# Retrieval look-ups with one operand in a PSUM bank

## Chip, cores and metric

One core of one Trainium2 chip runs the whole program. The metric is the device time of one execution in microseconds, as the median of several runs; lower is better.

## The reference

A decoder trunk of two layers over 256 tokens of width 1024, all in float32. Each layer has a mixer (a short convolution, then attention) and a product-key expert retrieval, which is what matters here:

```python
def chunk(xc):                                   # peer_ffn
    q = (xc @ w_q).reshape(PEER_CHUNK, PEER_HEADS, 2, PEER_HALF)        # 8 heads, 2 sides
    s1 = jnp.einsum('thd,nd->thn', q[:, :, 0], sub_k1)                  # 128 keys a side
    s2 = jnp.einsum('thd,nd->thn', q[:, :, 1], sub_k2)
    v1, i1 = lax.top_k(s1, PEER_TOPK)                                   # 16 of 128
    v2, i2 = lax.top_k(s2, PEER_TOPK)
    cand = (v1[..., :, None] + v2[..., None, :]).reshape(..., 256)
    cidx = (i1[..., :, None] * PEER_NKEYS + i2[..., None, :]).reshape(..., 256)
    top_s, top_pos = lax.top_k(cand, PEER_TOPK)                         # 16 of 256 pairs
    e_idx = jnp.take_along_axis(cidx, top_pos, axis=-1)
    g = jax.nn.softmax(top_s, axis=-1)
    u = u_emb[e_idx]                                                    # 16384 experts
    a = jax.nn.gelu(jnp.einsum('td,thkd->thk', xc, u))
    w = g * a
    return jnp.einsum('thk,thkd->td', w, v_emb[e_idx])
```

## The kernel before

The kernel doesn't gather experts. It multiplies the normed tokens with the whole table of experts, tile by tile, and puts gates on the result that are zero but for the chosen ones. The weights of the whole program form one list of items of 128 x 1024 float32; per layer there are 8 query tiles, then 128 tiles of u (the U stage) and 128 of v (the V stage). For exactness every operand is split into a high part and the remainder (the low part), and three products are summed.

An item passes through five engines. SyncE loads it (`issue`, L136). A u tile is turned by DVE (`turn_to`, L157), ACT rounds it to its high part (L171), POOL subtracts this in two halves of 512 columns to get the low part (`split_to`, L176), and PE multiplies (L880, L881 with the high part, L884 with the low part). There are three buffers of each kind, so a turn, a split and a load wait for the item three places earlier. For v tiles DVE makes the low part and nothing is turned.

The U stage has two halves. In items 0 to 63 (`WIDE`) an item is 24 matmuls of 256 columns into half a bank (L880, L881, L884), and after every odd item ACT evicts the pair's bank through a GELU (L1022). From item 64 on high and low token parts go in one matmul of 512 columns (L878), and the gate products (DVE L1070, L1078, L1092; PE L1085) run beside them, behind a gate in the order of work that opens only after item 63.

While items 0 to 61 run, DVE works out the retrieval in two batches of 128 tokens, called i = 0 and 1. This is written as a queue of side work: `add(cost, ...)` appends an instruction with a declared cost, and after each item `run_side(1.62)` gives 1.62 of credit and emits instructions while their cost is covered. Nearly all of it has line L215, since `add` calls it from there. The order per batch, all in `peer`: the key numbers of the 16 best of each side are cast to float16; numbers of side 1 are made into differences (`df`); five additions make 65 candidate sums (`cand`) from the side scores `v16`; the 16 largest are found with their positions `tp`; a shift by 4, a shift of 15 and a mask make the column within a block (`sh`, `tp[:, i, 1]`); both are cast to float16 (`pf`). Then each position is looked up by a one-hot: two compares of 2048 elements against `st16` and `io16` write `hot[i]`, a product of 4096 elements multiplies it with the table `tab` of key numbers, and `fold` (L939, three times) with a last addition sums over the 16 places. `tables(i)` lets ACT write that table beforehand: 2 x 2048 float16, each key number repeated 16 times (L933 to L935). At the end come the softmax of the gates, and `listed`, in which PE turns the lists (L995) and ACT evicts them (L999, L1000).

Bank `hi4[3]` (the last 2 KB of PSUM of each partition) is free from item 21 until the gate products keep their constants there from item 64 on: `hold` (L1065) copies them as words with a shift by 0, since the copy is to be bit for bit.

Of the kernel before, what the change touches and what calls it, by code (L numbers as in the profile page):

```python
# [12 lines left out]
F16 = mybir.dt.float16  # L13
BF16 = mybir.dt.bfloat16
I32 = mybir.dt.int32
U32 = mybir.dt.uint32
AF = mybir.ActivationFunctionType
OP = mybir.AluOpType
# [20 lines left out]
def trunk_kernel(ctx: ExitStack, tc, x, norm_mix, norm_ffn, conv_w_in, conv_w, conv_w_out,  # L39
# [3 lines left out]
    pe, dve, act, pool, sp = nc.tensor, nc.vector, nc.scalar, nc.gpsimd, nc.sync  # L43
# [15 lines left out]
    xbuf = sb.tile([128, 2560], F32, name="xbuf")  # L59
# [23 lines left out]
    def scratch(off, n):  # L83
        return big[:, off:off + n]
# [129 lines left out]
    def add(c, f, *a, gate=0, **k):  # L214
        side.append((c, lambda: f(*a, **k), gate))  # L215
# [42 lines left out]
    lo4, hi4 = B[0:4], B[4:8]  # L258
# [565 lines left out]
    def peer(l):  # L824
# [1 line left out]
        S = scratch(base, 4096).rearrange("p (b h s n) -> p b h s n", b=2, h=8, s=2)  # L826
        qT = scratch(80 * 256, 2048).rearrange("p (h t) -> p h t", t=256)
        qs = scratch(60 * 256, 1024).rearrange("p (t c) -> p t c", t=2)
        tab = xbuf[:, 0:2048].bitcast(F16).rearrange("p (g a n) -> p g a n", a=16, n=16)
        hot = [scratch(base + 2048 * i, 2048).bitcast(F16).rearrange("p (g a n) -> p g a n", a=16, n=16)  # L830
               for i in range(2)]
        o = base + 4096
        cand = scratch(o, 8 * 66).rearrange("p (h c) -> p h c", c=66)
        o += 528
        v16 = scratch(o, 512).rearrange("p (b h s n) -> p b h s n", b=2, h=8, s=2)
        i16 = scratch(o + 512, 512).bitcast(U32).rearrange("p (b s h n) -> p b s h n", b=2, h=8, s=2)
        if16 = scratch(o + 1024, 256).bitcast(F16).rearrange("p (b s h n) -> p b s h n", b=2, h=8, s=2)
        ts = scratch(o + 1280, 256).rearrange("p (b h n) -> p b h n", b=2, h=8)
        tp = scratch(o + 1536, 512).bitcast(U32).rearrange("p (b s h n) -> p b s h n", b=2, s=2, h=8)
        sh = scratch(o + 2048, 128).bitcast(U32).rearrange("p (h n) -> p h n", h=8)  # L840
        pf = scratch(o + 2176, 128).bitcast(F16).rearrange("p (s h n) -> p s h n", s=2, h=8)
        df = scratch(o + 2304, 64).bitcast(F16).rearrange("p (h n) -> p h n", h=8)
        f15 = scratch(o + 2368, 128).bitcast(U32).rearrange("p (h n) -> p h n", h=8)
        e12 = scratch(o + 2496, 512).rearrange("p (b s n) -> p b s n", b=2, s=2)
        gg = scratch(o + 3008, 256).rearrange("p (b h n) -> p b h n", b=2, h=8)
        gs = scratch(o + 3264, 16).rearrange("p (b h) -> p b h", b=2)
        io16 = scratch(o + 3280, 128).bitcast(F16).rearrange("p (a n) -> p a n", a=16)
        st16 = scratch(o + 3408, 128).bitcast(F16).rearrange("p (a n) -> p a n", a=16)
        kbd = scratch(o + 3536, 256)
# [70 lines left out]
        def topk(groups, cost):  # L920

            for lo in (0, 8):
                for v, m, p in groups:
                    add(cost, dve.max, m[:, lo:lo + 8], v)
                for v, m, p in groups:
                    add(cost, dve.max_index, p[:, lo:lo + 8], m[:, lo:lo + 8], v)
                if lo == 0:
                    for v, m, p in groups:
                        add(cost, dve.match_replace, v, m[:, 0:8], v, NEG)

        def tables(i):

            act.activation(df[:, :, 0:1], if16[:, i, 0, :, 0:1], AF.Copy)  # L933
            act.activation(tab[:, 8:16], if16[:, i, 1, :, :, None].to_broadcast([128, 8, 16, 16]), AF.Copy)
            act.activation(tab[:, 0:8], df[:, :, :, None].to_broadcast([128, 8, 16, 16]), AF.Copy)  # L935

        def fold(i, n):
            v = hot[i].rearrange("p g a n -> p g (a n)")
# [15 lines left out]
        q_out(1)  # L954
        for i in range(2):
            add(0.6, dve.tensor_copy, if16[:, i], i16[:, i])
            add(0.4, dve.tensor_tensor, df[:, :, 1:16], if16[:, i, 0, :, 1:16], if16[:, i, 0, :, 0:15],
                op=OP.subtract)
            for a0, n, first, width in ((0, 1, 0, 16), (1, 2, 16, 8), (3, 4, 32, 4), (7, 8, 48, 2), (15, 1, 64, 1)):
                add(0.4, dve.tensor_tensor,  # L960
                    cand[:, :, first:first + n * width].rearrange("p h (a c) -> p h a c", c=width),
                    v16[:, i, :, 0, a0:a0 + n, None].to_broadcast([128, 8, n, width]),
                    v16[:, i, :, 1, None, 0:width].to_broadcast([128, 8, n, width]), op=OP.add)
            for h in range(0, 8, 4):
                topk([(cand[:, h + a, 0:65], ts[:, i, h + a], tp[:, i, 0, h + a]) for a in range(4)], 0.25)
                if h == 0:
                    add(0.0, tables, i)
            add(0.4, dve.tensor_scalar, sh, tp[:, i, 0], 4, None, op0=OP.logical_shift_right)
            add(0.4, dve.tensor_tensor, sh, f15, sh, op=OP.logical_shift_right)
            add(0.4, dve.tensor_tensor, tp[:, i, 1], tp[:, i, 0], sh, op=OP.bitwise_and)  # L970
            add(0.6, dve.tensor_copy, pf, tp[:, i])
            add(1.4, dve.tensor_tensor, hot[i][:, 0:8], pf[:, 0, :, None, :].to_broadcast([128, 8, 16, 16]),
                st16[:, None].to_broadcast([128, 8, 16, 16]), op=OP.is_ge)
            add(1.4, dve.tensor_tensor, hot[i][:, 8:16], pf[:, 1, :, None, :].to_broadcast([128, 8, 16, 16]),
                io16[:, None].to_broadcast([128, 8, 16, 16]), op=OP.is_equal)
            add(2.5, dve.tensor_tensor, hot[i], hot[i], tab, op=OP.mult)
            for n in (8, 4, 2):
                add(0.3 + 0.14 * n, fold, i, n)
            add(0.6, dve.tensor_tensor, e12[:, i].rearrange("p s (h n) -> p (s h) n", h=8), hot[i][:, :, 0],
                hot[i][:, :, 1], op=OP.add)  # L980
            add(0.5, dve.tensor_tensor, gg[:, i], ts[:, i], ts[:, i, :, 0:1].to_broadcast([128, 8, 16]),
                op=OP.subtract)
        pause()
        add(0.0, act.activation, gg, gg, AF.Exp)
        add(0.8, dve.tensor_reduce, gs, gg, axis=AX.X, op=OP.add)
        add(0.2, dve.reciprocal, gs, gs)
        add(0.8, dve.tensor_tensor, gg, gg, gs[:, :, :, None].to_broadcast([128, 2, 8, 16]), op=OP.mult)
        lists = (B[4][:, 0:256], B[4][:, 256:512], B[5][:, 0:256])

        def listed():  # L990
# [214 lines left out]

    conv_mixer()
    peer(0)
    attn_mixer()
    peer(1)

# [32 lines left out]
```

## Time and profile before

| | |
|---|---|
| median of 3 runs | 1823.19 us (1821.16 to 1823.33) |
| the profiled execution | 1822.49 us; span 1820.7 us |
| busy: PE, PE weight load | 1797.7 us, 1573.6 us |
| busy: DVE, ACT, POOL | 1353.9 us, 894.6 us, 710.7 us |
| granted TensorE clock | 0.998 of full speed |
| U stage, items 0 to 63 | 137 to 334 us and 1053 to 1249 us |

The span runs from the first to the last instruction of the program; the execution's own time has 1.8 us around it. Busy time is the union of an engine's instructions. In the lists of instructions, a bracket at the end of a line is the idle time of the engine before it and who ended it. Instructions of the same kind that follow each other on one engine are merged into one line with a count.

### The profile page before, as it was taken

The numbers are of one execution on the slowest core, as the hardware profiler recorded it, in microseconds if no ns is written. First come the engines' busy times: TensorE is split into PE (matmuls) and PEld (weight loads), VectorE is DVE, ScalarE is ACT, GpSimd is POOL, SyncE is SP. The second block draws the span as 40 slices with busy tenths as digits, with TensorE's granted clock in tenths as the row PEclk, the third lists the DMA queues.
The fourth block names the chain that finished last, engine by engine and source line by source line (L and its number), as shares of the span: only waits on it lengthen the run. The fifth ranks groups of instructions, "written<-read, shape, count | busy, mean of one in ns | idle before, by whom it ended". The sixth has DMA issues, their size and how long they took to land.

```text
span 1820.7 us, 32357 instructions
## 1 busy us (share of the span) xinstructions
PE 1797.7 (99%) x11985; PEld 1573.6 (86%) x11985; DVE 1353.9 (74%) x2183; ACT 894.6 (49%) x1109; POOL 710.7 (39%) x549
## 2 busy tenths in 40 slices
PE   9999999999999999999999999999999999999998
PEld 8979999988888888888788799999888888888886
DVE  4748888788888887555567487887888898875555
ACT  5455445555454444544454554545455544445443
POOL 1048899978820000000200388999888300000000
PEclk9999999999999999999999999999999999999999
DMA  7566655665555555655562675556565555556564
GB/s 210 154 194 188 183 163 168 175 178 168 172 161 183 166 173 183 227 193 194 163 184 86 174 205 169 166 169 183 165 172 167 160 185 174 174 174 228 191 194 138
DMA packets 204581, 321.15 MB, mean 176 GB/s; under 512 B 26221, under 2 KB 157317, under 8 KB 203910
## 3 DMA queue, kind: packets, MB, share of 16 engines
q1 hardware_dynamic: 202006, 312.33, 56.2%
q10 hardware_dynamic: 2416, 6.75, 1.1%
q8 instruction: 94, 1.54, 0.4%
q14 instruction: 65, 0.53, 0.1%
HBM read 315.83 MB, written 3.15 MB: 175 GB/s over the span
## 4 chain that ended last, share of the span: by engine, by line
PE 90%; DVE 4%; DMA 2%; ACT 1%; POOL 1%; issue 1%; SPq 0%; DVEq 0%; ACTq 0%; POOLq 0%
PE psum L485 41%; PE psum L878 13%; PE psum L884 12%; PE psum L880 5%; PE psum L881 5%; PE psum L1085 3%; PE psum L472 3%; PE psum L518 2%; DVE big L215 1%; POOL lo L176 1%; DVE tr L157 1%; PE psum L916 1%; DVE lo L176 1%; DMA raw<-in_conv_w_out_dram 1%; ACT hi L171 1%
## 5 line engine op out<-in xcount | busy, mean ns | idle before, releaser
L176 POOL TENSOR_TENSOR lo<-tr,hi 128x512 fp32r<-128x512 f32 x496 | 652.3, 1348 | 109.4 <-ACT hi L171 104.8
L176 DVE TENSOR_TENSOR lo<-raw,hi 128x1024 fp32r<-128x1024 f32 x316 | 388.1, 1229 | 259.1 <-ACT hi L171 253.1
L171 ACT ACTIVATE hi<-raw 128x1024 fp32r<-128x1024 f32 x331 | 349.7, 1060 | 448.4 <-PE psum L485 365.4
L485 PE MATMUL psum<-hi,x 128*128 128x512 f32 x2208 | 553.0, 392 | 0.7 <-ACT hi L171 0.7
L485 PEld LDWEIGHTS psum<-hi,x 128*128 128x128 f32 x2208 | 409.0, 188 | 82.6 <-ACT hi L171 1.1
L157 DVE STREAM_TRANSPOSE tr<-raw 128x1024 f32<-128x1024 f32 x256 | 316.0, 1234 | 64.2 <-POOL lo L176 38.2
L171 ACT ACTIVATE hi<-tr 128x1024 fp32r<-128x1024 f32 x256 | 270.3, 1058 | 128.4 <-DVE tr L157 113.5
L884 PE MATMUL psum<-x,lo 128*128 128x256 f32 x2048 | 292.0, 283 | 6.2 <-POOL lo L176 6.2
L485 PE MATMUL psum<-lo,x 128*128 128x512 f32 x1104 | 295.2, 389 | 0.4 <-POOL lo L176 0.4
L884 PEld LDWEIGHTS psum<-x,lo 128*128 128x128 f32 x2048 | 273.6, 191 | 18.6 <-POOL lo L176 8.6
L176 POOL TENSOR_TENSOR lo<-raw,hi 128x512 fp32r<-128x512 f32 (+1 forms) x27 | 49.1, 1848 | 609.5 <-ACT hi L171 557.3
L878 PE MATMUL psum<-x,hi 128*128 128x512 f32 x1024 | 263.6, 398 | 0.0
L880 PE MATMUL psum<-x,hi 128*128 128x256 f32 x1024 | 252.7, 284 | 0.8 <-ACT hi L171 0.8
L881 PE MATMUL psum<-x,hi 128*128 128x256 f32 x1024 | 251.1, 283 | 0.0
L485 PEld LDWEIGHTS psum<-lo,x 128*128 128x128 f32 x1104 | 207.1, 188 | 43.9 <-POOL lo L176 0.8
L878 PEld LDWEIGHTS psum<-x,hi 128*128 128x128 f32 x1024 | 183.6, 189 | 33.3
L880 PEld LDWEIGHTS psum<-x,hi 128*128 128x128 f32 x1024 | 196.3, 192 | 1.5 <-ACT hi L171 1.2
L881 PEld LDWEIGHTS psum<-x,hi 128*128 128x128 f32 x1024 | 196.4, 192 | 0.2
L1185 POOL TENSOR_TENSOR big<-xbuf,big 128x256 f32<-128x256 f32 x2 | 1.4, 732 | 383.4 <-DVE rstd L348 383.4
L1070 DVE TENSOR_TENSOR xbuf<-psum,eT 128x1536 f16<-128x1536 f16 x128 | 119.9, 937 | 10.1 <-PE psum L1085 10.1
L1040 ACT ACTIVATE big<-psum 128x512 f32<-128x512 f32 x64 | 38.2, 597 | 125.6 <-PE psum L884 125.6
L1022 ACT ACTIVATE big<-psum 128x512 f32<-128x512 f32 x64 | 38.1, 596 | 115.6 <-PE psum L884 115.5
(164 smaller groups left out, 1573.4 us busy)
## 6 DMA issues: line engine op xcount, KB each, us to landing
raw<-in_peer_u_dram SPq DMA_DIRECT2D x1024, 128.0 KB, 3.0
raw<-in_peer_v_dram SPq DMA_DIRECT2D x256, 512.0 KB, 4.2
raw<-in_conv_w_in_dram SPq DMA_DIRECT2D x96, 128.0 KB, 2.6
raw<-in_attn_w_qkv_dram SPq DMA_DIRECT2D x96, 128.0 KB, 2.7
raw<-in_peer_w_q_dram SPq DMA_DIRECT2D x64, 128.0 KB, 2.9
raw<-in_conv_w_out_dram SPq DMA_DIRECT2D x8, 512.0 KB, 4.2
raw<-in_attn_w_o_dram SPq DMA_DIRECT2D x8, 512.0 KB, 3.7
x_dram<-xbuf ACTq DMA_DIRECT2D x2, 1024.0 KB, 4.8
```

The lines of the kernel that those rows point to most:

```text
L157: dve.transpose(TR[m % 3].rearrange("p b (g i) -> p g b i", g=4), RAW[m % 3].rearrange("p (g m) -> p g m", m=256))
L171: act.activation(HI[m % 3], src, AF.Copy)
L176: eng.tensor_sub(LO[m % 3][:, c], src[:, c], HI[m % 3][:, c])
L472: pe.matmul(banks[c // 2][:, (c % 2) * 256:(c % 2) * 256 + 256], w[:, c * 128:c * 128 + 128], xx[:, b], start=(b == 0 and p == 0 and c % 2 ...
L485: pe.matmul(banks[j], x[:, j // 2 * 128:j // 2 * 128 + 128], w[:, j % 2 * 512:j % 2 * 512 + 512], start=(first and p == 0), stop=(last and ...
L878: pe.matmul(o, w, X2[:, b], start=(b == 0), stop=False, skip_group_check=True)
L880: pe.matmul(o, w, XH[:, b], start=(b == 0), stop=False)
L881: pe.matmul(o, w, XL[:, b], start=False, stop=False)
L884: pe.matmul(o[:, 0:256], lo[:, b * 128:b * 128 + 128], XH[:, b], start=False, stop=(b == 7), skip_group_check=(o.shape[-1] == 512))
L1040: act.activation(A[:, k - 1:k + 1], halves(k, 1), AF.Copy)
L1070: dve.tensor_tensor(HOT[s % 2].rearrange("p b (r k) t -> p b r k t", r=3), numbers[:, None, None].to_broadcast([128, TOK // 2, 3, 64, 2]), ...
L1085: pe.matmul(o, pairs[:, t // 2, :, t % 2], OHG[s % 2][:, a, t // 2, :, t % 2], start=(a == 0), stop=(a == 1))
```

## The change

What is read by several look-ups is copied into bank `hi4[3]`, so that a DVE instruction has one operand in PSUM and one in SBUF: the positions (`picks`), the key numbers (`values`), the scores of the second side (`side1`), the shifts (`sh`) and the reciprocals of the softmax (`gr`). The positions and the key numbers go there as 32-bit words by a shift of 0 (`words`). ACT's table of 4096 float16 gives way to one in which each number stands twice (`vp`, 512 float16): ACT writes 8 x 2 and 8 x 16 x 2 elements of it, DVE the differences, and the product reads the pairs with a broadcast over a middle dimension. `xbuf` holds two of these tables, one a batch.

```diff
--- before.py
+++ after.py
@@ -826,7 +826,7 @@
         S = scratch(base, 4096).rearrange("p (b h s n) -> p b h s n", b=2, h=8, s=2)
         qT = scratch(80 * 256, 2048).rearrange("p (h t) -> p h t", t=256)
         qs = scratch(60 * 256, 1024).rearrange("p (t c) -> p t c", t=2)
-        tab = xbuf[:, 0:2048].bitcast(F16).rearrange("p (g a n) -> p g a n", a=16, n=16)
+        vp = [xbuf[:, 256 * i:256 * i + 256].bitcast(F16).rearrange("p (g a r) -> p g a r", a=16, r=2) for i in range(2)]
         hot = [scratch(base + 2048 * i, 2048).bitcast(F16).rearrange("p (g a n) -> p g a n", a=16, n=16)
                for i in range(2)]
         o = base + 4096
@@ -837,13 +837,17 @@
         if16 = scratch(o + 1024, 256).bitcast(F16).rearrange("p (b s h n) -> p b s h n", b=2, h=8, s=2)
         ts = scratch(o + 1280, 256).rearrange("p (b h n) -> p b h n", b=2, h=8)
         tp = scratch(o + 1536, 512).bitcast(U32).rearrange("p (b s h n) -> p b s h n", b=2, s=2, h=8)
-        sh = scratch(o + 2048, 128).bitcast(U32).rearrange("p (h n) -> p h n", h=8)
         pf = scratch(o + 2176, 128).bitcast(F16).rearrange("p (s h n) -> p s h n", s=2, h=8)
-        df = scratch(o + 2304, 64).bitcast(F16).rearrange("p (h n) -> p h n", h=8)
         f15 = scratch(o + 2368, 128).bitcast(U32).rearrange("p (h n) -> p h n", h=8)
         e12 = scratch(o + 2496, 512).rearrange("p (b s n) -> p b s n", b=2, s=2)
         gg = scratch(o + 3008, 256).rearrange("p (b h n) -> p b h n", b=2, h=8)
         gs = scratch(o + 3264, 16).rearrange("p (b h) -> p b h", b=2)
+
+        sh = hi4[3][:, 0:128].bitcast(U32).rearrange("p (h n) -> p h n", h=8)
+        picks = hi4[3][:, 0:128].bitcast(F16).rearrange("p (s h n) -> p s h n", s=2, h=8)
+        values = hi4[3][:, 128:384].bitcast(F16).rearrange("p (g a r) -> p g a r", a=16, r=2)
+        side1 = hi4[3][:, 384:512].rearrange("p (h n) -> p h n", h=8)
+        gr = hi4[3][:, 384:400].rearrange("p (b h) -> p b h", b=2)
         io16 = scratch(o + 3280, 128).bitcast(F16).rearrange("p (a n) -> p a n", a=16)
         st16 = scratch(o + 3408, 128).bitcast(F16).rearrange("p (a n) -> p a n", a=16)
         kbd = scratch(o + 3536, 256)
@@ -928,11 +932,14 @@
                     for v, m, p in groups:
                         add(cost, dve.match_replace, v, m[:, 0:8], v, NEG)
 
+        def words(dst, src):
+
+            dve.tensor_scalar(dst, src, 0, None, op0=OP.logical_shift_right)
+
         def tables(i):
 
-            act.activation(df[:, :, 0:1], if16[:, i, 0, :, 0:1], AF.Copy)
-            act.activation(tab[:, 8:16], if16[:, i, 1, :, :, None].to_broadcast([128, 8, 16, 16]), AF.Copy)
-            act.activation(tab[:, 0:8], df[:, :, :, None].to_broadcast([128, 8, 16, 16]), AF.Copy)
+            act.activation(vp[i][:, 0:8, 0], if16[:, i, 0, :, 0:1].to_broadcast([128, 8, 2]), AF.Copy)
+            act.activation(vp[i][:, 8:16], if16[:, i, 1, :, :, None].to_broadcast([128, 8, 16, 2]), AF.Copy)
 
         def fold(i, n):
             v = hot[i].rearrange("p g a n -> p g (a n)")
@@ -954,13 +961,14 @@
         q_out(1)
         for i in range(2):
             add(0.6, dve.tensor_copy, if16[:, i], i16[:, i])
-            add(0.4, dve.tensor_tensor, df[:, :, 1:16], if16[:, i, 0, :, 1:16], if16[:, i, 0, :, 0:15],
-                op=OP.subtract)
+            add(0.4, dve.tensor_tensor, vp[i][:, 0:8, 1:16], if16[:, i, 0, :, 1:16, None].to_broadcast([128, 8, 15, 2]),
+                if16[:, i, 0, :, 0:15, None].to_broadcast([128, 8, 15, 2]), op=OP.subtract)
+            add(0.3, dve.tensor_copy, side1, v16[:, i, :, 1])
             for a0, n, first, width in ((0, 1, 0, 16), (1, 2, 16, 8), (3, 4, 32, 4), (7, 8, 48, 2), (15, 1, 64, 1)):
                 add(0.4, dve.tensor_tensor,
                     cand[:, :, first:first + n * width].rearrange("p h (a c) -> p h a c", c=width),
                     v16[:, i, :, 0, a0:a0 + n, None].to_broadcast([128, 8, n, width]),
-                    v16[:, i, :, 1, None, 0:width].to_broadcast([128, 8, n, width]), op=OP.add)
+                    side1[:, :, None, 0:width].to_broadcast([128, 8, n, width]), op=OP.add)
             for h in range(0, 8, 4):
                 topk([(cand[:, h + a, 0:65], ts[:, i, h + a], tp[:, i, 0, h + a]) for a in range(4)], 0.25)
                 if h == 0:
@@ -969,11 +977,15 @@
             add(0.4, dve.tensor_tensor, sh, f15, sh, op=OP.logical_shift_right)
             add(0.4, dve.tensor_tensor, tp[:, i, 1], tp[:, i, 0], sh, op=OP.bitwise_and)
             add(0.6, dve.tensor_copy, pf, tp[:, i])
-            add(1.4, dve.tensor_tensor, hot[i][:, 0:8], pf[:, 0, :, None, :].to_broadcast([128, 8, 16, 16]),
+            add(0.3, words, hi4[3][:, 0:128].bitcast(U32), pf.rearrange("p s h n -> p (s h n)").bitcast(U32))
+            add(0.4, words, hi4[3][:, 128:384].bitcast(U32), vp[i].rearrange("p g a r -> p (g a r)").bitcast(U32))
+            add(1.4, dve.tensor_tensor, hot[i][:, 0:8], picks[:, 0, :, None, :].to_broadcast([128, 8, 16, 16]),
                 st16[:, None].to_broadcast([128, 8, 16, 16]), op=OP.is_ge)
-            add(1.4, dve.tensor_tensor, hot[i][:, 8:16], pf[:, 1, :, None, :].to_broadcast([128, 8, 16, 16]),
+            add(1.4, dve.tensor_tensor, hot[i][:, 8:16], picks[:, 1, :, None, :].to_broadcast([128, 8, 16, 16]),
                 io16[:, None].to_broadcast([128, 8, 16, 16]), op=OP.is_equal)
-            add(2.5, dve.tensor_tensor, hot[i], hot[i], tab, op=OP.mult)
+            pairs = hot[i].rearrange("p g a (n r) -> p g a n r", r=2)
+            add(2.5, dve.tensor_tensor, pairs, pairs, values[:, :, :, None, :].to_broadcast([128, 16, 16, 8, 2]),
+                op=OP.mult)
             for n in (8, 4, 2):
                 add(0.3 + 0.14 * n, fold, i, n)
             add(0.6, dve.tensor_tensor, e12[:, i].rearrange("p s (h n) -> p (s h) n", h=8), hot[i][:, :, 0],
@@ -983,8 +995,8 @@
         pause()
         add(0.0, act.activation, gg, gg, AF.Exp)
         add(0.8, dve.tensor_reduce, gs, gg, axis=AX.X, op=OP.add)
-        add(0.2, dve.reciprocal, gs, gs)
-        add(0.8, dve.tensor_tensor, gg, gg, gs[:, :, :, None].to_broadcast([128, 2, 8, 16]), op=OP.mult)
+        add(0.2, dve.reciprocal, gr, gs)
+        add(0.8, dve.tensor_tensor, gg, gg, gr[:, :, :, None].to_broadcast([128, 2, 8, 16]), op=OP.mult)
         lists = (B[4][:, 0:256], B[4][:, 256:512], B[5][:, 0:256])
 
         def listed():
```

## Rows read from the trace of the kernel before

**Rows 1.** The page, busy time of each engine, whole span.

```profile
PE 1797.7 (99%) x11985; PEld 1573.6 (86%) x11985; DVE 1353.9 (74%) x2183; ACT 894.6 (49%) x1109; POOL 710.7 (39%) x549
```

**Rows 2.** Waits of PE, whole span: us in total, times, longest us.

```profile
PE psum L884 <- POOL lo L176: 6.2, 8, 1.4
```

**Rows 3.** ACT in order of time, first layer: start us, us, instruction.

```profile
258.48 0.60 ACT L1022 ACTIVATE big<-psum 128x512 f32<-128x512 f32 x1 [2.78 <-PE psum L884]
...
264.45 0.60 ACT L1022 ACTIVATE big<-psum 128x512 f32<-128x512 f32 x1 [2.99 <-PE psum L884]
...
284.36 1.90 ACT L934 ACTIVATE xbuf<-big 128x2048 f16<-128x2048 f16 x1
...
287.96 2.00 ACT L171 ACTIVATE hi<-tr 128x1024 fp32r<-128x1024 f32 x2
...
295.37 0.60 ACT L1022 ACTIVATE big<-psum 128x512 f32<-128x512 f32 x1 [1.28 <-PE psum L884]
...
301.13 0.60 ACT L1022 ACTIVATE big<-psum 128x512 f32<-128x512 f32 x1 [0.59 <-PE psum L884]
...
309.31 0.60 ACT L1022 ACTIVATE big<-psum 128x512 f32<-128x512 f32 x1 [2.98 <-PE psum L884]
...
315.85 0.60 ACT L1022 ACTIVATE big<-psum 128x512 f32<-128x512 f32 x1 [1.41 <-PE psum L884]
```

**Rows 4.** ACT in order of time, second layer.

```profile
1173.96 0.60 ACT L1022 ACTIVATE big<-psum 128x512 f32<-128x512 f32 x1 [2.78 <-PE psum L884]
...
1231.22 0.60 ACT L1022 ACTIVATE big<-psum 128x512 f32<-128x512 f32 x1 [1.41 <-PE psum L884]
```

**Rows 5.** POOL grouped, 194:222, 241.8:278, 340:500 (busy us, mean ns | idle); then one operation.

```profile
L176 POOL TENSOR_TENSOR lo<-tr,hi 128x512 fp32r<-128x512 f32 x19 | 24.1, 1300 | 5.2 <-ACT hi L171 5.2
...
L176 POOL TENSOR_TENSOR lo<-tr,hi 128x512 fp32r<-128x512 f32 x24 | 36.6, 1561 | 2.1 <-ACT hi L171 2.1
...
L176 POOL TENSOR_TENSOR lo<-tr,hi 128x512 fp32r<-128x512 f32 x105 | 132.6, 1294 | 28.8 <-ACT hi L171 28.8
...
260.24 3.38 POOL L176 TENSOR_TENSOR lo<-tr,hi 128x512 fp32r<-128x512 f32 x1
```

**Rows 6.** DVE in order of time, first layer: start us, us, instruction.

```profile
260.21 2.25 DVE L215 TENSOR_TENSOR big<-big,xbuf 128x4096 f16<-128x4096 f16 x1
...
273.00 4.10 DVE L215 TENSOR_TENSOR big<-big 128x120 f16<-128x120 f16 x4
...
278.18 0.33 DVE L215 TENSOR_TENSOR big<-big 128x128 f32<-128x128 f32 x2
```

**Rows 7.** DVE grouped by shape, whole span: count | busy us, mean ns | idle.

```profile
L157 DVE STREAM_TRANSPOSE tr<-raw 128x1024 f32<-128x1024 f32 x256 | 316.0, 1234 | 64.2 <-POOL lo L176 38.2 <-DMA raw<-in_peer_u_dram 24.2 <-ACT big L1022 1.3
...
L1070 DVE TENSOR_TENSOR xbuf<-psum,eT 128x1536 f16<-128x1536 f16 x128 | 119.9, 937 | 10.1 <-PE psum L1085 10.1
...
L1078 DVE TENSOR_TENSOR xbuf<-xbuf,psum 128x1024 f16<-128x1024 f16 x128 | 85.9, 671 | 1.3
...
L215 DVE TENSOR_TENSOR big<-big 128x128 f32<-128x128 f32 x20 | 18.5, 958 | 0.0
...
L215 DVE TENSOR_TENSOR big<-big 128x2048 f16<-128x2048 f16 x8 | 9.4, 1176 | 0.0
...
L215 DVE TENSOR_TENSOR big<-big,xbuf 128x4096 f16<-128x4096 f16 x4 | 9.0, 2249 | 0.0
...
L215 DVE TENSOR_TENSOR big<-big 128x128 uint32<-128x128 uint32 x8 | 6.1, 762 | 0.1
...
L215 DVE TENSOR_TENSOR big<-psum,big 128x256 f32<-128x256 f32 x16 | 5.9, 413 | 0.0
...
L215 DVE TENSOR_TENSOR big<-psum,big 128x512 f32<-128x512 f32 x8 | 5.5, 683 | 0.0
...
L1065 DVE TENSOR_SCALAR psum<-gT 128x256 uint32<-128x256 uint32 x4 | 1.7, 428 | 0.1
```

**Rows 8.** DVE in order of time, last of the gate products, first layer.

```profile
516.50 1.28 DVE L1092 SCALAR_TENSOR_TENSOR big<-psum,big 128x512 f32<-128x512 f32 x2
```

## Prediction

> **What bounds the kernel now.** I read the busy shares first: PE is busy 99% of the span [rows 1]. So only time in which PE stands still can be saved. PE's waits come next: the largest is the low-part products (L884) waiting for POOL's low parts (L176), 6.2 us in 8 times [rows 2]. A pipelined PE hides part of a wait in its busy time, so I measure the stall itself by the rhythm of the U stage. In its first 64 items each item is 24 matmuls, and after every second item ACT evicts the pair's bank with a GELU (L1022). That eviction waits for PE, so the spacing of its starts is the pace of PE. Undisturbed it is 5.76 us a pair, 2.88 an item: 295.37 to 301.13 [rows 3]. From 258.48 to 315.85 are nine pairs: 57.37 us against 51.84, **5.53 us of stall** [rows 3]. The second layer has 1173.96 to 1231.22, also nine pairs: 57.26, **5.42 us** [rows 4]. Together 10.95 us. This is the stretch of the look-ups, and the same work in both layers.
>
> Where the 5.53 lies [rows 3]: 0.21 to 264.45; 30.92 less 28.80 = 2.12 to 295.37; none to 301.13; 2.42 to 309.31; 0.78 to 315.85. There are two causes.
>
> POOL. It splits every U tile in two operations of 1.30 us, 2.6 of an item's 2.88 us. In a stretch without look-ups its 19 operations stay at 1300 ns and leave 5.2 us idle; in the look-ups of the first batch 24 operations take 1561 ns each and POOL is never free but for 2.1 us ahead of them [rows 5]. One of these shows why: 3.38 us, starting at 260.24 [rows 5], 0.03 us after DVE's 2.25 us product of one-hot and table started [rows 6]; 1.30 + 2.25 less a small overlap. The two engines take turns, and it works both ways: DVE's three additions of side scores at 273.00 belong to a group of four that takes 4.10 us, one POOL operation each, while the two at 278.18, with POOL idle, take 0.33 [rows 6]. All of these read both operands from SBUF. With one operand in PSUM it is otherwise: from 340 to 500 us DVE builds its gate products with a PSUM operand (L1070, L1078 [rows 7]), and 105 POOL operations beside them stay at 1294 ns [rows 5].
>
> ACT. It fills the two halves of the table, 1.90 us each, from 284.36, so the high part behind them starts at 287.96 with no idle time before it [rows 3]. It is two tiles' high parts, 1.0 us each, and PE can start its next item only when the first is there: tables of 3.6 us stand where otherwise nothing would. I put about 1.0 of the 2.12 us down to this.
>
> **The change part by part, per batch (there are four: two of 128 tokens in each of two layers).**
>
> Positions and key numbers in PSUM. The two compares keep their elements (1.18 us each), the product too (2.25) [rows 7]. The nearest rows of the new form are L1070, 1536 elements in 937 ns, and L1078, 1024 in 671: 0.52 ns for each further element [rows 7]. That gives 671 + 1024 x 0.52 = 1.20 us for a compare and 671 + 3072 x 0.52 = 2.27 for the product: DVE gains nothing in its own time. Lower end 2.25 as now; upper end the pace of float32 instructions, (683 - 413)/256 = 1.05 ns an element [rows 7], or 2.30 and 4.46. I take the fast value, since L1078 has the very form of the new product: pairs from PSUM, spread over a middle dimension. POOL however is no longer held: 2 x 1.18 + 2.25 = 4.6 us less a few tenths of overlap, about 4.2 of the 6.3 us (24 x 0.26) that it loses in the first stretch [rows 5].
>
> Side scores and shifts in PSUM. Five additions of up to 128 elements go from about 0.96 us [rows 7] to at most the 413 ns of a 256-element form and at least the 0.16 of the two at 278.18 [rows 6]; I take 0.28. That is 4.1 to 1.3 us. Two shift and mask instructions go from 762 ns [rows 7] to the same 0.28, a further 1.0 saved. The softmax scale at the end does not bear on the stall.
>
> Added on DVE: two copies of words into PSUM, one of 256 words (428 ns [rows 7]), one of 128 (between 0.21 and 0.43 as half and whole of that; 0.28), a copy of 128 side scores (same bounds, 0.28), and a difference of twice the elements (+0.13 us by 120 elements at 1.05). Together 1.1 us against 3.8 saved. They write PSUM from one SBUF source, so POOL should not be held; if it is, 1 us of POOL time a batch comes back. Nobody waits for them but the next DVE instruction, and behind that the next transpose.
>
> ACT's table shrinks from 4096 to 272 elements: 3.8 us to between 0.3 and 0.7 (by elements from 1.90 us for 2048, and with a fixed part). The high part behind it starts 3 us sooner. PE's 1.0 us goes.
>
> What moves. The look-ups are paced by declared costs, 1.62 an item. The three added instructions declare 1.0 a batch, 2.0 in all, so the listing slips by 1.2 items: counted through the queue from after item 61 to after item 62, and the closing gate instruction to after 63. The hold of the next stage may not run before then in either kernel, so that stage starts in the same item. Its cover, if it did not: the last gate products of the first layer are multiplied in at 516.50 [rows 8]; by the queue that is after item 122, five items before the last of the stage. ACT's seven list evictions move by an item with it, at no cost. SP and POOL get no instruction more or less, and no DMA changes.
>
> What is late next. The folds (L939), the casts and the final sums still read SBUF alone. Each pair of them still lets a POOL operation in between, and the transposes of the next tiles stand behind them in DVE's queue. POOL still loses about 2 us a batch there (6.3 less 4.2). In the clean stretch it is idle 5.2 us of some 29, in ten items [rows 5], which gives 0.5 us back an item, or some 4 us over the eight items that hold these instructions, and it no longer begins the batch behind, as the 2.1 us wait on ACT now makes it do [rows 5]. So I expect the rest to be covered: residual 0 to 1 us a batch, taken at 0.15, 0.6 in all.
>
> **Sum:** 10.95 - 0.6 = 10.4 us. The profiled execution took 1822.49 us (span 1820.7): 1812.1. The median of the runs is 0.7 above it: **1812.8 us**, 0.57% less. A time within 0.2% (3.6 us) is what a measurement of this kernel can hardly tell from no change.
>
> **Rivals.**
>
> A. The folds keep half the stall. For it: the stall of 0.78 after 309.31 lies at folds alone, and fold and cast still hold POOL 2 us a batch. Against: the lead above. Price: 1 us a batch left, 4 in all: 1823.2 - 6.9 = 1816.3. Chance 0.20.
>
> B. Nothing is gained: the instructions are slowed by POOL as before although an operand is in PSUM, or DVE, relieved, still delivers the transposes late. Against it: 1294 ns beside PSUM operands [rows 5]. Time 1822 to 1824. Chance 0.07.
>
> C. Slower: a two-operand instruction with float16 from PSUM runs at one element per 1.05 ns here, since here the destination is read as well. Place: DVE, two compares and a product in a row. Price: 2 x 1.1 + 2.2 = 4.4 us a batch. They declare 5.3, so 3.3 items or 9.4 us, and would need 2.30 + 2.30 + 4.46 + 3.3 transposes of 1.23 [rows 7] = 13.1: 3.7 late, with the folds 4.7. It decides once DVE is later than its lead; with no lead it costs 4 x 4.7 = 19 against 11 saved, 1831; with half of it hidden about 1822. I put it at 1827. Against it: 0.52 ns an element in L1070 and L1078. Chance 0.04. The Trainium skill's "VectorE: DVE Perf Modes", section "The perf-mode tier table", speaks for this case: it lists tensor_tensor with any PSUM operand at the base rate of one element a cycle, and by it the time would be that of this rival. This trace's rows with 937 and 671 ns disagree with that table, and the same page, under "Why PSUM operands drop a tier", allows two a cycle.
>
> **How the numbers follow.** The forecast has 0.69 with 1810.0 to 1814.5: from every stall gone and a microsecond of scatter, to half the residual bound. A takes in 1814.5 to 1819. The range 1810.0 to 1819 holds these two, and leaves out B, C and a little on either side. Faster by over 0.2%: 0.69 + 0.19 = 0.88 (A's slow end goes to the same). Same 0.08, slower 0.04.
>
> **What would show it.** In the profile after, the GELU evictions in both stretches should stand 5.76 us apart, but for a few tenths at the folds. POOL's operations in the look-ups should fall from 1561 to about 1380 ns and its busy time by some 17 us; DVE's by some 11 (4 x 2.7); ACT's by 13 (4 x 3.3). The product should take 2.3 us. The PE wait L884 on POOL should vanish. I am wrong if the product takes over 4 us, if POOL operations beside the new compares last 2.3 us, or if pairs stay at 6 to 8 us behind late transposes. Stages after the look-ups should keep their lengths; if the saving is given back there, something else than PE paced them.

## The result, and the profile after

The changed kernel takes 1812.26 us (median of 4 runs, 1810.24 to 1812.6) against 1822.47 for the kernel before (4 runs, one more than in the table above): a ratio of 0.9942, 95% interval 0.9925 to 0.9959, that is 10.2 us or 0.56% less. The profiled execution took 1812.53 us, 9.96 less than the one of before.

The page, busy times:

```profile
span 1810.7 us, 32361 instructions
...
PE 1795.5 (99%) x11985; PEld 1574.2 (87%) x11985; DVE 1347.8 (74%) x2195; ACT 881.6 (49%) x1105; POOL 693.5 (38%) x549
```

ACT in order of time, the GELU evictions of the first layer (now L1034; start us, us, instruction, idle time before it):

```profile
259.65 0.60 ACT L1034 ACTIVATE big<-psum 128x512 f32<-128x512 f32 x1 [2.78 <-PE psum L888]
...
294.21 0.60 ACT L1034 ACTIVATE big<-psum 128x512 f32<-128x512 f32 x1 [2.78 <-PE psum L888]
299.97 0.60 ACT L1034 ACTIVATE big<-psum 128x512 f32<-128x512 f32 x1 [2.78 <-PE psum L888]
305.73 0.60 ACT L1034 ACTIVATE big<-psum 128x512 f32<-128x512 f32 x1 [2.78 <-PE psum L888]
...
329.43 0.60 ACT L1034 ACTIVATE big<-psum 128x512 f32<-128x512 f32 x1
```

The same of the second layer, first and last of the stretch:

```profile
1169.35 0.60 ACT L1034 ACTIVATE big<-psum 128x512 f32<-128x512 f32 x1 [2.78 <-PE psum L888]
...
1239.12 0.60 ACT L1034 ACTIVATE big<-psum 128x512 f32<-128x512 f32 x1
```

And of the kernel before, the evictions after items 61 and 63 of the first layer, between which the lists are turned, and the one after item 63 of the second:

```profile
327.38 0.60 ACT L1022 ACTIVATE big<-psum 128x512 f32<-128x512 f32 x1 [1.70 <-PE psum L884]
333.79 0.60 ACT L1022 ACTIVATE big<-psum 128x512 f32<-128x512 f32 x1 [1.93 <-PE psum L884]
...
1249.17 0.60 ACT L1022 ACTIVATE big<-psum 128x512 f32<-128x512 f32 x1 [1.93 <-PE psum L884]
```

Where rows 3 had spacings of 5.97, 8.18 and 6.54 us, every pair of the look-ups now takes 5.76. To compare kernels whose lists are turned one item earlier or later, all stalls from here on are measured over the twelve pairs from the eviction after item 39 to that after item 63. Undisturbed these take 12 x 5.76 us and 0.65 for turning the lists (333.79 - 327.38 = 6.41 for that pair of the kernel before), 69.77. The changed kernel has 329.43 - 259.65 = 69.78 and 1239.12 - 1169.35 = 69.77: no stall. The kernel before has 333.79 - 258.48 = 75.31 and 1249.17 - 1173.96 = 75.21, **5.54 and 5.44 us** of stall. The sum, 10.98, is the whole gain. The profiled spans differ by 10.0 since the changed one reached the eviction after item 39 of the first layer 1.17 us later (259.65 against 258.48); at the first eviction of the stage, ahead of the changed instructions, it was already 1.32 us later (146.48 against 145.16), and over the kernels below the start of the stretch varies from 257.4 to 259.8. Outside the two stretches nothing is given back: from the first to the second are 840.2 us before and 839.9 after, from the last row to the end of the span 571.5 and 571.6.

POOL, grouped: the stretch without look-ups, then the first batch (busy us, mean ns | idle before):

```profile
L176 POOL TENSOR_TENSOR lo<-tr,hi 128x512 fp32r<-128x512 f32 x19 | 24.1, 1299 | 5.2 <-ACT hi L171 5.2
...
L176 POOL TENSOR_TENSOR lo<-tr,hi 128x512 fp32r<-128x512 f32 x26 | 35.0, 1379 | 3.0 <-ACT hi L171 3.0
```

The second answers to rows 5: 1561 ns has become 1379. And DVE by shape (count | busy us, mean ns | idle):

```profile
L215 DVE TENSOR_TENSOR big<-psum,big 128x2048 f16<-128x2048 f16 x8 | 9.5, 1185 | 0.0
L946 DVE TENSOR_TENSOR big<-big 128x2048 f16<-128x2048 f16 x4 | 9.3, 2317 | 0.0
L215 DVE TENSOR_TENSOR big<-big,psum 128x4096 f16<-128x4096 f16 x4 | 9.0, 2249 | 0.0
...
L215 DVE TENSOR_TENSOR xbuf<-big 128x240 f16<-128x240 f16 x4 | 5.5, 1386 | 0.1
...
L215 DVE TENSOR_TENSOR big<-big,psum 128x128 f32<-128x128 f32 x16 | 3.5, 268 | 0.1
...
L937 DVE TENSOR_SCALAR psum<-xbuf 128x256 uint32<-128x256 uint32 x4 | 1.7, 428 | 0.1
...
L215 DVE TENSOR_TENSOR psum<-big,psum 128x128 uint32<-128x128 uint32 x4 | 1.2, 296 | 0.1
```

PE's waits now begin with one that is not of this stage; L888 (L884 before) on POOL is gone:

```profile
PE psum L372 <- DVE big L367: 1.6, 4, 0.4
```

### The profile page after: what moved, and what is told of

Read it like the earlier page. It is cut to its first block, busy times and chain, and to the rows that moved or that the text cites. A ratio compares the mean times of both kernels' runs of the same rounds, so it can differ in the third digit from the quotient of the medians.

```text
span 1810.7 us, 32361 instructions
## 1 busy us (share of the span) xinstructions
PE 1795.5 (99%) x11985; PEld 1574.2 (87%) x11985; DVE 1347.8 (74%) x2195; ACT 881.6 (49%) x1105; POOL 693.5 (38%) x549
## 4 chain that ended last, share of the span: by engine, by line
PE 94%; DVE 2%; DMA 1%; ACT 1%; POOL 1%; issue 0%; SPq 0%; DVEq 0%; ACTq 0%; POOLq 0%
PE psum L485 41%; PE psum L888 14%; PE psum L882 13%; PE psum L885 7%; PE psum L884 7%; PE psum L1097 4%; PE psum L472 3%; PE psum L518 2%; PE psum L920 1%; DVE lo L176 1%; DMA raw<-in_conv_w_out_dram 1%; POOL lo L176 1%; PE psum L492 0%; PE psum L493 0%; PE psum L494 0%; ACT hi L171 0%
## 5 line engine op out<-in xcount | busy, mean ns | idle before, releaser
L176 POOL TENSOR_TENSOR lo<-tr,hi 128x512 fp32r<-128x512 f32 x496 | 635.0, 1313 | 115.7 <-ACT hi L171 115.4
L888 PE MATMUL psum<-x,lo 128*128 128x256 f32 x2048 | 288.6, 283 | 0.0
L888 PEld LDWEIGHTS psum<-x,lo 128*128 128x128 f32 x2048 | 272.6, 191 | 9.8
L884 PE MATMUL psum<-x,hi 128*128 128x256 f32 x1024 | 252.6, 284 | 0.0
L884 PEld LDWEIGHTS psum<-x,hi 128*128 128x128 f32 x1024 | 196.5, 192 | 0.2
L1034 ACT ACTIVATE big<-psum 128x512 f32<-128x512 f32 x64 | 38.3, 598 | 141.0 <-PE psum L888 141.0
```

The costliest lines, as they stand in the source:

```text
L176: eng.tensor_sub(LO[m % 3][:, c], src[:, c], HI[m % 3][:, c])
L884: pe.matmul(o, w, XH[:, b], start=(b == 0), stop=False)
L888: pe.matmul(o[:, 0:256], lo[:, b * 128:b * 128 + 128], XH[:, b], start=False, stop=(b == 7), skip_group_check=(o.shape[-1] == 512))
L1034: act.activation(a, a if k >= WIDE[l] else lo4[(k // 2) % 4], AF.Gelu)
```

## The experiments

Three theories. **P**, of the prediction: where both operands lie in SBUF, DVE and POOL take turns, and the PSUM operand ends that. **T**: what counts is ACT's smaller table. **Q**: the added copies declare 1.0 more a batch, so the queue spaces its instructions wider, and that gives the time. The prediction also had a lead: POOL and DVE may fall behind by some microseconds before PE notices. All edits start from the changed kernel, except those marked as of the kernel before. Stall is that of the first and the second layer, in the one profiled execution of each kernel; time is the median of its runs.

| kernel | read from SBUF, or changed | stall, us | time, us | ratio to before, 95% interval |
|---|---|---|---|---|
| before | everything | 5.54, 5.44 | 1822.47 | |
| changed | nothing | 0.01, 0.00 | 1812.26 | 0.9942 (0.9925 to 0.9959) |
| e1_sbuf | additions, shifts, compares, product | 3.69, 6.35 | 1821.32 | 0.9996 (0.9986 to 1.0006) |
| e2_table | large table written too | 0.01, 0.00 | 1810.95 | 0.9940 (0.9924 to 0.9957) |
| e3_side | additions, shifts | 0.01, 0.00 | 1811.46 | 0.9943 (0.9926 to 0.9959) |
| e8_both | additions, shifts, and large table | 0.01, 0.00 | 1810.53 | 0.9940 (0.9923 to 0.9956) |
| e6_prod | product | 0.00, 0.00 | 1811.55 | 0.9943 (0.9927 to 0.9960) |
| e7_comp | compares | 0.01, 0.00 | 1811.03 | 0.9939 (0.9922 to 0.9955) |
| e4_look | compares, product | 3.17, 3.22 | 1816.86 | 0.9973 (0.9962 to 0.9983) |
| e9_cast | compares, product; cast from PSUM | 0.94, 0.93 | 1813.77 | 0.9952 (0.9935 to 0.9968) |
| e10_prod_side | additions, shifts, product | 3.03, 3.03 | 1815.18 | 0.9963 (0.9949 to 0.9977) |
| e5_pace | copies declared at 0 | 0.00, 0.01 | 1811.38 | 0.9937 (0.9920 to 0.9953) |
| b1_pace (of before) | 1.0 a batch declared for nothing | 5.60, 5.60 | 1822.80 | 1.0000 (0.9990 to 1.0009) |
| b2_table (of before) | small table | 5.71, 5.07 | 1821.61 | 0.9992 (0.9982 to 1.0002) |

**e1_sbuf.** Every copy into PSUM is still made, but its readers go to SBUF:

```diff
-        sh = hi4[3][:, 0:128].bitcast(U32).rearrange("p (h n) -> p h n", h=8)
+        sh = scratch(o + 2048, 128).bitcast(U32).rearrange("p (h n) -> p h n", h=8)
...
-                    side1[:, :, None, 0:width].to_broadcast([128, 8, n, width]), op=OP.add)
+                    v16[:, i, :, 1, None, 0:width].to_broadcast([128, 8, n, width]), op=OP.add)
...
-            add(1.4, dve.tensor_tensor, hot[i][:, 0:8], picks[:, 0, :, None, :].to_broadcast([128, 8, 16, 16]),
+            add(1.4, dve.tensor_tensor, hot[i][:, 0:8], pf[:, 0, :, None, :].to_broadcast([128, 8, 16, 16]),
...
-            add(1.4, dve.tensor_tensor, hot[i][:, 8:16], picks[:, 1, :, None, :].to_broadcast([128, 8, 16, 16]),
+            add(1.4, dve.tensor_tensor, hot[i][:, 8:16], pf[:, 1, :, None, :].to_broadcast([128, 8, 16, 16]),
...
-            add(2.5, dve.tensor_tensor, pairs, pairs, values[:, :, :, None, :].to_broadcast([128, 16, 16, 8, 2]),
+            add(2.5, dve.tensor_tensor, pairs, pairs, vp[i][:, :, :, None, :].to_broadcast([128, 16, 16, 8, 2]),
```

> The changed kernel, with every copy into PSUM still made and paid for, but the additions, the shifts, the compares and the product read their operands from SBUF. Theory P (where both operands lie in SBUF, DVE and POOL take turns; the PSUM operand ends that): POOL's operations in the first batch's look-ups are back near 1560 ns, and of the 10.95 us of stall in the two layers 7 to 10 return, all but ACT's part; 1819 to 1822 us. Theory T (the smaller table on ACT is what counts): at most 2 us return; 1812 to 1814. Theory Q (the 1.0 more of declared cost a batch spaces the instructions out): none returns; 1812.

POOL in the first batch, and PE's largest wait:

```profile
L176 POOL TENSOR_TENSOR lo<-tr,hi 128x512 fp32r<-128x512 f32 x23 | 35.4, 1574 | 1.4 <-ACT hi L171 1.4
```

```profile
PE psum L888 <- POOL lo L176: 4.3, 6, 1.4
```

In the profiled execution 3.69 + 6.35 = 10.0 of the 11.0 us are back and the time is that of the kernel before, though instructions, their order, their declared costs and ACT's small table are those of the changed one. T and Q fall as explanations of the whole; the place that the operands are read from makes the difference. The two layers differ by 2.7 us: in the second the shift of the second batch took 5.15 us, of which more below; in the first, with 3.69 us, no instruction waited so long.

**e2_table, e3_side, e8_both.** ACT writes the old table as well, to a place that nothing reads (`big_tab` is `xbuf[:, 512:2560]`); side scores and shifts come from SBUF (the first two pieces of e1_sbuf); both together:

```diff
+            act.activation(big_tab[:, 8:16], if16[:, i, 1, :, :, None].to_broadcast([128, 8, 16, 16]), AF.Copy)
+            act.activation(big_tab[:, 0:8], if16[:, i, 0, :, :, None].to_broadcast([128, 8, 16, 16]), AF.Copy)
             act.activation(vp[i][:, 0:8, 0], if16[:, i, 0, :, 0:1].to_broadcast([128, 8, 2]), AF.Copy)
```

> The changed kernel, and ACT writes the two large halves of the old table as well, which nothing reads. Theory P: about 1 us a layer returns, behind the second table where the next high part starts late, and at most 1 us a layer more at the folds, since POOL then begins the first batch 2 us behind: 2 to 4 us in all, 1814 to 1816. Theory T: 9 to 11 us return, 1821 to 1823. Theory Q: none.

> The changed kernel with side scores and shifts read from SBUF, the look-ups still from PSUM. The five additions are back at about 0.96 us each, DVE is 3 to 4 us busier a batch, POOL loses little. Theory P as predicted (DVE's transposes have a lead that covers this): 0 to 1.5 us return, 1812 to 1814. If late transposes behind the additions make the stall: 4 us or more return, 1816 and up.

> The changed kernel with the large table written again by ACT and the side scores and shifts read from SBUF; only the look-ups have a PSUM operand. Each alone returned nothing. Theory P: the look-ups' operands are what counts, 0 to 1.5 us a layer return; 1811 to 1815. If table and side scores together are what stalled the kernel before: 2 us or more a layer.

The work is there, in e2_table on ACT and in e3_side on DVE:

```profile
L942 ACT ACTIVATE xbuf<-big 128x2048 f16<-128x2048 f16 x4 | 7.6, 1900 | 0.0
L943 ACT ACTIVATE xbuf<-big 128x2048 f16<-128x2048 f16 x4 | 7.6, 1900 | 0.0
```

```profile
L215 DVE TENSOR_TENSOR big<-big 128x128 f32<-128x128 f32 x20 | 13.3, 702 | 0.0
```

Nothing comes back, of either or of both. For e2_table the expectation of P, 2 to 4 us, was a miss: 3.8 us of ACT in front of a high part do no harm here, where the transposes are in time. So as long as the look-ups have a PSUM operand, neither the small table nor the side scores and shifts in PSUM are worth anything that can be measured.

**e6_prod, e7_comp, e4_look.** The product from SBUF; the compares from SBUF; both (the pieces of e1_sbuf for each).

> The changed kernel with the product alone reading its table of pairs from SBUF; compares, side scores and shifts from PSUM. With compares and product in SBUF 3.2 us a layer came back (e4_look), 0.2 after the first batch and 3.0 after the second. Lead theory (POOL's loss counts only beyond a lead): one product costs POOL 2.1 us, the lead takes most of it, 0 to 1.3 us a layer return. Proportion theory (each us that POOL loses delays PE by the same part): 1.6 us a layer.

> The changed kernel with the two compares alone reading positions from SBUF; product, side scores and shifts from PSUM. Lead theory: 2 x 1.0 us of POOL, 0 to 1.2 us a layer return, and this and e6_prod together less than the 3.2 us a layer of both at once. Proportion theory: 1.6 us a layer, the two together 3.2.

> The changed kernel with compares and product read from SBUF, side scores and shifts from PSUM. POOL is held for 4.2 us a batch again. Theory P: the first batch of a layer mostly lives on POOL's lead, the second does not: 2 to 3.5 us a layer return, 4 to 7 in all, 1816 to 1819. Theory T: under 1 us.

One POOL operation beside the product in e6_prod, and one beside a compare in e7_comp:

```profile
303.64 3.41 POOL L176 TENSOR_TENSOR lo<-tr,hi 128x512 fp32r<-128x512 f32 x1
```

```profile
296.08 2.28 POOL L176 TENSOR_TENSOR lo<-tr,hi 128x512 fp32r<-128x512 f32 x1
```

POOL is held for 2.1 and 1.0 us again (3.41 and 2.28 against 1.30), and PE doesn't notice: the proportion theory falls, the lead covers either. Both together return 3.2 us a layer, inside the range expected; but the trace of e4_look shows that this is not the held POOL alone. DVE, then POOL, in the second batch:

```profile
295.18 1.25 DVE L157 STREAM_TRANSPOSE tr<-raw 128x1024 f32<-128x1024 f32 x1
296.35 0.25 DVE L215 TENSOR_TENSOR big<-big,psum 128x128 uint32<-128x128 uint32 x1
296.63 5.16 DVE L215 CAST big<-big 128x256 f16<-128x256 uint32 x1
...
302.49 1.23 DVE L157 STREAM_TRANSPOSE tr<-raw 128x1024 f32<-128x1024 f32 x1
```

```profile
279.00 22.64 POOL L176 TENSOR_TENSOR lo<-tr,hi 128x512 fp32r<-128x512 f32 x18 [0.17 <-ACT hi L171]
304.89 8.11 POOL L176 TENSOR_TENSOR lo<-tr,hi 128x512 fp32r<-128x512 f32 x4 [3.25 <-ACT hi L171]
```

A cast that takes 0.3 us when alone stood 5.16 us while POOL ran on without a gap, and ended 0.15 us after POOL had run out of tiles at 301.64. The next transpose came 7.3 us after the last, and POOL then waited 3.25 us for its input. In the second layer the same cast took 5.60 us.

**e9_cast** takes that cast out of the way: as e4_look, but the positions are copied as words into PSUM and cast from there. What it has beyond e4_look:

```diff
-            add(0.6, dve.tensor_copy, pf, tp[:, i])
+            tq = hi4[3][:, 128:384].bitcast(U32)
+            add(0.0, words, tq, tp[:, i].rearrange("p s h n -> p (s h n)"))
+            add(0.6, dve.tensor_copy, pf.rearrange("p s h n -> p (s h n)"), tq)
```

> As e4_look (compares and product from SBUF), but the positions go through PSUM on their way to the cast, so that the cast has its source there. In e4_look one cast a layer took 5.16 and 5.60 us instead of 0.3 to 1.4, through four POOL operations, and the stall began behind it. Cast theory: the casts take under 0.6 us, and of e4_look's 6.4 us at most 2 remain; 1811 to 1813. Lead theory alone (the compares and the product use up POOL's lead whatever the cast does): 4 us or more remain, 1815 and up.

```profile
1206.71 0.42 DVE L215 CAST big<-psum 128x256 f16<-128x256 uint32 x1
...
1208.99 4.04 DVE L215 TENSOR_TENSOR big<-big 128x2048 f16<-128x2048 f16 x1
1212.96 1.23 DVE L157 STREAM_TRANSPOSE tr<-raw 128x1024 f32<-128x1024 f32 x1
```

The casts take 0.42 us, and of 6.4 us of stall 1.9 remain: 4.5 us of e4_look were the cast's wait. The time, 1813.77, is still 0.8 us above the range of the cast theory. What is left goes with the compares and the product, which hold POOL as in e4_look and wait themselves: the compare of these rows, 1.18 us alone, took 4.04, that of the first layer 3.08.

**e10_prod_side.** Product, additions and shifts from SBUF, compares from PSUM.

> The changed kernel with the product, the side scores and the shifts read from SBUF, only the compares from PSUM. Alone, product and side scores cost nothing (e6_prod, e3_side). Lead theory: POOL's 2.1 us and DVE's 3 us a batch draw on the same lead, and 0 to 2 us a layer return. If each part is harmless in itself: nothing returns.

```profile
293.41 5.17 DVE L215 TENSOR_SCALAR big<-big 128x128 uint32<-128x128 uint32 x1
```

3.0 us a layer are back, more than the lead theory allowed. Here it is the first shift, 0.18 us at its shortest, that stood 5.17 us behind POOL, 5.05 in the second layer, and POOL then stood without input for 2.9 us in either. In the changed kernel this shift writes to PSUM and takes 0.28 us. So shifts in PSUM are worth nothing while the rest is in PSUM, and with additions and product from SBUF the one that waits longest is a shift left in SBUF. Additions from SBUF beside the product, with the shifts in PSUM, were not run, so what part of the 3.0 us is the additions' is not shown.

**e5_pace, b1_pace.** The three copies of the changed kernel declared at 0; in the kernel before, 0.3 and 0.7 declared for nothing at the same places.

```diff
-            add(0.3, dve.tensor_copy, side1, v16[:, i, :, 1])
+            add(0.0, dve.tensor_copy, side1, v16[:, i, :, 1])
...
-            add(0.3, words, hi4[3][:, 0:128].bitcast(U32), pf.rearrange("p s h n -> p (s h n)").bitcast(U32))
-            add(0.4, words, hi4[3][:, 128:384].bitcast(U32), vp[i].rearrange("p g a r -> p (g a r)").bitcast(U32))
+            add(0.0, words, hi4[3][:, 0:128].bitcast(U32), pf.rearrange("p s h n -> p (s h n)").bitcast(U32))
+            add(0.0, words, hi4[3][:, 128:384].bitcast(U32), vp[i].rearrange("p g a r -> p (g a r)").bitcast(U32))
```

> The changed kernel with the three added copies declared at 0, so that the queue runs at the pace of the kernel before: the listing comes after item 61 again. Theory P: no stall returns, within 0.3 us a layer; 1811 to 1813. Theory Q (the later pace gave the time): several us return.

> The kernel before with 1.0 us a batch of declared cost for nothing, in the places where the changed kernel has its copies: 0.3 ahead of the additions, 0.7 ahead of the compares. Theory Q: most of the 10.95 us goes, 1812 to 1815. Theory P: DVE and POOL meet as before; the stall stays within 2 us of what it was, 1820 to 1823.

No stall in the one, 5.60 us a layer in the other: Q falls from both sides.

**b2_table.** The kernel before with the table of pairs in SBUF, as ACT and the difference write it in the changed kernel, and the product over pairs.

```diff
...
-            add(2.5, dve.tensor_tensor, hot[i], hot[i], tab, op=OP.mult)
+            pairs = hot[i].rearrange("p g a (n r) -> p g a n r", r=2)
+            add(2.5, dve.tensor_tensor, pairs, pairs, vp[i][:, :, :, None, :].to_broadcast([128, 16, 16, 8, 2]),
+                op=OP.mult)
```

> The kernel before with the small table of pairs alone, in SBUF, every operand read from SBUF and nothing added. ACT's 3.8 us a batch are gone. Theory T as it stands in the prediction: about 1 us a layer goes, and another 0 to 1 by POOL's earlier start: 1819 to 1821. If e2_table holds here too (ACT's table costs nothing): within 0.5 us a layer, 1821 to 1823.

```profile
291.12 4.50 DVE L215 TENSOR_SCALAR big<-big 128x128 uint32<-128x128 uint32 x1
```

ACT, the evictions after items 39 and 51 of the first layer:

```profile
257.56 0.60 ACT L1023 ACTIVATE big<-psum 128x512 f32<-128x512 f32 x1 [2.78 <-PE psum L884]
...
292.81 0.60 ACT L1023 ACTIVATE big<-psum 128x512 f32<-128x512 f32 x1 [1.34 <-PE psum L884]
```

The total hardly moved, 5.71 and 5.07 us, and the median is within 0.2% of before. But the shift of the second batch stood 4.50 and 4.38 us in the two layers, which it does not in the kernel before. Up to item 51, where that wait has not yet reached PE, six pairs took 35.25 us, a stall of 0.69, where the kernel before had 36.89 (258.48 to 295.37 in rows 3), a stall of 2.33; in the second layer 0.71 and 2.21. So the small table and what goes with it saved 1.6 and 1.5 us up to there, and the new wait took it back. The runs point the same way: four of ten took 1817.5 to 1818.8 us, less than any of the 14 of the kernel before beside them (1820.7 and up), and six 1821.3 to 1823.8. That the four went without the long wait is a guess, since none of them was profiled; with the shift out of the way the small table was not tried.

No version is faster than the changed kernel: those without stall lie between 1810.5 and 1812.3 us, within each other's intervals.

## Why the prediction was right, and where not

**What bounds the kernel, and the size.** The stall of nine pairs, 10.95 us, was the bound of the gain, and 10.98 went. The forecast of 10.4, 1812.8 us, held, at 1812.26. Rivals A (half the stall stays at the folds) and B (nothing) did not come.

**The mechanism.** e1_sbuf shows it alone: with the same work, PSUM or SBUF as the place of the operand is 10 us, by estimate some 7.4 without the long wait of one shift (twice the first layer's 3.69). The forecasts for single rows held: compares 1.20 predicted and 1185 ns measured, product 2.27 and 2249 ns, POOL's operations 1380 and 1379 ns, POOL's busy time 17 us less (710.7 to 693.5), ACT's 13 (894.6 to 881.6), additions 0.28 and 268 ns, copies of words 0.43 and 428, 0.28 and 280.

**Rival C** was one element per 1.05 ns. 4096 elements in 2249 ns are 0.55 ns each, so the measurement decides against it. The Trainium skill's "VectorE: DVE Perf Modes" lists the base rate for tensor_tensor with any operand in PSUM under "The perf-mode tier table"; that does not hold for these float16 operands.

**DVE's share of the sum was mis-sized.** Some 11 us less were predicted; DVE is busy 6.1 us less (1353.9 to 1347.8). The additions and shifts fell by no less than forecast. But I took what still reads SBUF alone at its old durations plus the new elements. The difference of 240 elements takes 1386 ns where 694 plus 130 were expected, and the first fold went from 1692 to 2317 ns: these two now meet a POOL operation each time. The second fold (647 to 1156 ns) and the last addition (377 to 890) meet one in two of their four places. None of them delays PE.

**The step on ACT failed.** "PE's 1.0 us goes" because the table shrinks: e2_table writes the large table again and nothing returns. The high part stood behind the table, as read, but beside look-ups that read PSUM the large table costs PE nothing: those operands alone end this stall too. In the kernel before the table did have a price: b2_table lost some 1.5 us a layer less up to item 51, of the order of the 1.0 that I read, though 0.7 stayed. So one stall had two causes, and their parts do not add up.

**The step on side scores and shifts** counted 3.8 us of DVE a batch saved. e3_side shows that PE gains nothing by it while the look-ups read PSUM. The residual of 0.15 us a batch at the folds was 0, as the lead argument had it.

**The lead** was right for one held resource at a time (e6_prod, e7_comp: 0), and for both with the cast out of the way nearly so (e9_cast: 0.93 a layer). But e4_look fell into its range for a reason that I had not thought of, the long wait of a cast (last section). This fits a kernel before that stalled by held POOL operations, waiting additions and late tables together; how its 11 us divide among them stays open, since the parts don't add up.

## What to carry to other kernels

Measure a stall by the rhythm of a regular stage, not by the waits listed: here it gave 10.95 us as the bound, and the time fell by 10.2. Beside an elementwise engine that is busy nine tenths of the time, give DVE's instructions one operand, or the result, in PSUM, the long ones first; here that took both engines out of each other's way (POOL's operations from 1561 to 1379 ns). Where buffers give a lead, causes don't add: undoing one of several may cost nothing, and removing one of several may gain nothing.

## What the runs showed of the hardware that was not expected

I had counted on turns: a DVE instruction waits for at most one POOL operation. Most do (1.39 us and less for a cast of 0.25). The Trainium skill's "SBUF — State Buffer", section "Who interferes with whom", likewise has the later of two block until the first has finished, and the 3.38 us of rows 5 agree. But seven of the casts and shifts from SBUF to SBUF in all these profiles took 4.4 to 5.6 us: POOL went on with up to four further operations that were ready, and DVE came in when POOL ran dry. It also befell instructions with two operands, though for less (3.08 and 4.04 us in e9_cast for 1.18). All of these were in the second batch, with POOL running without a gap; yet the kernel before ran POOL without a gap there too and none of its casts stood longer than 1.38 us. In which cases POOL keeps the turn is open. The two kernels with such a wait and most of the old stall also scatter more (b2_table 1817.5 to 1823.8, e1_sbuf 1817.7 to 1824.8 us). In the changed kernel the casts, folds, differences and sums still have all operands in SBUF and could meet it; in its profile the longest of them is a fold of 2.33 us.
